# Encoder layer on one core: the second half-step's way out in seven products, its stream normed ahead by halves

## The chip, the core and the metric

One Trainium2 core runs the whole layer as one program. The metric is the time of an execution on the device in microseconds; the time before is the median of three runs. TensorE (PE) multiplies, VectorE (DVE) and ScalarE (ACT) work elementwise, GpSimd (POOL) and SyncE (SP) issue transfers (DMA) between HBM and the on-chip memory; a transfer that POOL issues may add to what lies at its destination.

## The reference

The layer works on 528 tokens (16 meta tokens ahead of 512) of width 1024; a half-step's inner width is 2816.

```python
h = concatenate([meta, x])
h = h + 0.5 * swiglu(rms_norm(h, norm_ffn1), w_ffn1_in, w_ffn1_out)
u = rms_norm(h, norm_mix) @ w_in
y = concatenate([rms_norm(rg_lru(...) * gelu(gate)), rms_norm(fourier_mix(...))])
h = h + y @ w_out
h = h + 0.5 * swiglu(rms_norm(h, norm_ffn2), w_ffn2_in, w_ffn2_out)
return rms_norm(h, norm_final)[16:]

def swiglu(h, w_in, w_out):
    gate, up = split(h @ w_in, 2)
    return (silu(gate) * up) @ w_out
```

## The kernel before

Everything lies transposed: a tile holds 128 channels by up to 528 tokens; the stream `h` is 8 such tiles. Each product of float32 numbers is done as three matmuls of split numbers (`mm3`, L240 to 246): high by high, high by low, low by high. The high part of a weight is a copy by ScalarE (L88, L221), the low part what VectorE leaves of it (L89, L222).

**Way in.** A half-step goes over 22 blocks `f` of 128 inner channels. Blocks 0 and 1 of the second are classic: 8 gate and 8 up tiles against the 8 tiles of the stream, in matmuls of 512 tokens. The others (`pair`, L398) take gate and up, and both halves of the tokens, as a 2 by 2 product and do it in seven products instead of eight, each of 4 tiles in matmuls of 256 tokens. The sums of tokens for this are made once (`sums_of_x`). The sums of weights are made per block: `pair_loads` fills raw tiles a (up, 512 KB), b (gate, 512 KB) and c (up's first half, 256 KB) by SP (L103, L104, L105), and POOL adds a half of gate onto b (L106) and the other onto c (L107). `pair_blocks` splits a, then VectorE adds c's first half onto b's second (L118) and makes c's second half (L119) from a and b:

```python
split_w(jh, jl, b[:, 512:])
nc.vector.tensor_tensor(b[:, 512:], b[:, 512:], c[:, :512], op=ALU.add)
nc.vector.tensor_tensor(c[:, 512:], a[:, 512:], b[:, 512:], op=ALU.add)
```

Raw tiles come from a pool of 7 buffers (`wraw`), split ones from 5 (`wsp`). A list of jobs gives the order of the weights; a job is split 3 ahead of its use and loaded 6 ahead. The normalisation's factor R is multiplied onto gate and up afterwards (L437, L439), as the weights don't depend on it; while it is found (`roots_of`, `rstd_of`: sums L337, root L348, reciprocal L349, spread L355), TensorE works on block 0.

**Way out.** The blocks go out in chunks (`CHUNKS2`, 4, 5, 5, 4, 4): for each of 8 output blocks d one load, one split (L221, L222), 3 matmuls of 512 tokens per block (`po`, L242 to 246) and one addition onto the stream (L517). The outputs of a chunk lie between the blocks of the next (`ffn_steps`). The last chunk is the `tail`, by groups of 256 tokens, with the final normalisation. Ahead of the half-step stands the output projection (`WOUT`, 8 steps with `pw`, L848 to 868).

The order of instructions on each engine, and the buffer that each tile gets, are set by a scheduler from the program's order; at run time every engine works its list strictly in order, and so do SP and POOL with their transfers.

Of the kernel before, what the change touches and what calls it, by code (L numbers as in the profile page):

```python
# [14 lines left out]
P = 128  # L15
D = 1024
# [10 lines left out]
CHUNKS2 = [4, 5, 5, 4, 4]  # L27
# [11 lines left out]
CS_V = [1, 2, 3]  # L39
ROOT_M = 7  # L40
# [23 lines left out]
def encoder_layer(ctx: ExitStack, tc: tile.TileContext, xT, vecs, w1i, w1o, wm, wg, wo, w2i, w2o,  # L64
# [4 lines left out]
    wraw = ctx.enter_context(tc.tile_pool(name="wraw", bufs=7))  # L69
# [63 lines left out]

    def parts_given(src):
# [14 lines left out]
    def ffn_steps(chunks, late):  # L149

        steps, f0, prev = [], 0, None
        for c in chunks:
            for i in range(c):
                steps.append(("in", f0 + i, None))
                if prev:
                    steps += [("out", prev, d) for d in range(*(max(0, ND - (c - k) * ND // c - late) if k < c else ND for k in (i, i + 1)))]
            prev = (f0, f0 + c)
            f0 += c
        return steps + [("out", prev, d) for d in range(ND)]

    STEPS1, STEPS2 = ffn_steps(CHUNKS1, 0), ffn_steps(CHUNKS2, 1)

    def ffn_jobs(wi, wo_, steps, classic):
        for kind, f, d in steps:
            if kind == "out":
                jobs.append((wo_[d][:, f[0]:f[1], :], P, f[1] - f[0], P, 8))
            elif f in classic:
                for b in range(2):
                    jobs.append((wi[f, b], P, 8, P, 2 if len(jobs) < 3 else 8))
            else:  # L170
                pair = {"src": (wi[f, 1], wi[f, 0])}
                for part in (pair_blocks, pair_sums, pair_differences):
                    jobs.append((part, pair))

    ffn_jobs(w1i, w1o, STEPS1, CLASSIC1)
# [10 lines left out]
    ffn_jobs(w2i, w2o, STEPS2, CLASSIC2)  # L186
# [13 lines left out]
    def fetch(i):  # L200
# [5 lines left out]
        elif jobs[i][0] is pair_blocks:  # L206
            pair_loads(jobs[i][1])

# [99 lines left out]
    def sums_of_x(pool, g, t0, n, k):  # L308
        m = n // 2
        a, b = h[k][:, t0:t0 + n], h[k + 4][:, t0:t0 + n]  # L310
        z = pool.tile([P, 5, HT], F32, tag="q", name="z")
        t1, t2, t3, t4, xg = [z[:, i, :m] for i in range(5)]
        nc.scalar.activation(xg, a[:, :m], AF.Copy, scale=vec(g, k))
        nc.vector.scalar_tensor_tensor(t1, a[:, m:], less(g, k), xg, op0=ALU.mult, op1=ALU.add)
        nc.vector.scalar_tensor_tensor(t2, b[:, m:], less(g, k + 4), t1, op0=ALU.mult, op1=ALU.subtract)
        nc.vector.scalar_tensor_tensor(t3, t2, -1.0, xg, op0=ALU.mult, op1=ALU.subtract)
        nc.vector.scalar_tensor_tensor(t4, b[:, :m], less(g, k + 4), t2, op0=ALU.mult, op1=ALU.subtract)
# [3 lines left out]
        return th, tl  # L321

# [17 lines left out]
    def rstd_of(q, name):  # L340
        r = tmp.tile([P, T], F32, tag="rstd", name=name)
# [26 lines left out]
    def ffn(X, g, ss, t0, n, steps, classic, on_done, tail, lead=None):  # L368
        st = {"R": ss} if lead else {}
        half = n // 2  # L370
        with tc.tile_pool(name="ffn", bufs=10) as fp, tc.tile_pool(name="ffnt", bufs=2) as ft:
# [3 lines left out]
            def sums_ready():  # L375
                if not XT:
                    XT.extend(sums_of_x(ft, g, t0, n, k) for k in range(4))

            if not lead:
                sums_ready()  # L380

            def activated(u):
                ah = fp.tile([P, T], F32R, tag="ah", name="ah")
                al = fp.tile([P, T], F32R, tag="al", name="al")
                split_to(ah[:, :n], al[:, :n], u)
                return ah, al
# [7 lines left out]
            def onto(ps, w, x, first):  # L394

                for k in range(4):
                    xh, xl = x(k)
                    mm3([ps], w[0][:, k], w[1][:, k], [xh], [xl], first and k == 0, k == 3, True)  # L398
# [3 lines left out]
            def pair(f, R):  # L402

                def new():
                    return bank("pp")[:, :half]

                add = ALU.add
                q = ft.tile([P, 5, HT], F32, tag="q", name="q")
                q0, q1, q2, u0, u1 = [q[:, i, :half] for i in range(5)]
                a11, a12, a22 = block()  # L410
                A = new()
                onto(A, a11, b(0, 0), True)
                nc.scalar.activation(q0, A, AF.Copy)  # L413
                ps = new()
                onto(ps, a12, b(1, 0), True)
                nc.vector.tensor_tensor(q0, q0, ps, op=add)
                yield
                s1, s2 = block()
                onto(A, s2, t(1), False)
                nc.scalar.activation(u0, A, AF.Copy)  # L420
                yield
                s3, s4 = block()
                C = new()
                onto(C, s3, t(2), True)
                onto(A, s1, t(0), False)
                nc.scalar.activation(q2, A, AF.Copy)
                nc.vector.tensor_tensor(u1, q2, C, op=add)
                yield
                onto(A, s4, b(1, 1), False)

                yield
                onto(C, a22, t(3), False)
                nc.vector.tensor_tensor(u0, u0, C, op=add)

                Rv = like2(R)
                uv, gv = q[:, :2, :half], q[:, 3:, :half]
                nc.vector.tensor_tensor(gv, gv, Rv, op=ALU.mult)  # L437
                nc.scalar.activation(gv, gv, AF.Silu, scale=-1.0)
                nc.vector.tensor_tensor(gv, gv, Rv, op=ALU.mult)  # L439
                nc.vector.tensor_tensor(q0, q0, u0, op=ALU.mult)  # L440
                nc.vector.tensor_tensor(q1, A, u1, op=ALU.mult)
                ah = fp.tile([P, T], F32R, tag="ah", name="ah")
                al = fp.tile([P, T], F32R, tag="al", name="al")
                split_to(like2(ah), like2(al), uv)
                acts[f] = ah, al

            late = []

            def interleaved(f, R):

                gen = pair(f, R)
                for _ in range(3):
                    next(gen)
                    if late:
                        next(late[0], None)
                if late:
                    late.pop()
                late.append(gen)

            def finish_late():  # L460
                while late:
                    for _ in late.pop():
                        pass

            def like2(x):
                return x[:, :n].rearrange("p (a b) -> p a b", a=2)

            def gate_up(pg, pu):
                R = st["R"]
                q = ft.tile([P, 5, HT], F32, tag="q", name="q").rearrange("p a b -> p (a b)")  # L470
                g, u = q[:, :T], q[:, T:2 * T]
                times(g, pg, R, n)
                nc.scalar.activation(g[:, :n], g[:, :n], AF.Silu)
                times(u, pu, R, n)
                nc.vector.tensor_tensor(u[:, :n], u[:, :n], g[:, :n], op=ALU.mult)
                return activated(u[:, :n])
# [8 lines left out]
            acts = {}  # L485
            for kind, f, d in steps:
                if kind == "in" and f not in classic:
                    interleaved(f, st["R"])
                elif kind == "in":
                    finish_late()  # L490
                    if lead and f == 0:
                        ps = lead[:2]
                    else:
# [3 lines left out]
                        if "R" in st:  # L497
                            project(ps[1])
                        else:
                            q = roots_of(ss, n, D)  # L500
                            project(ps[1], lambda: st.update(R=rstd_of(q, "r")))
                    acts[f] = gate_up(*ps)
                    sums_ready()
                elif f[1] == NF and tail is not None:
                    finish_late()
                    tail([acts[j] for j in range(*f)], ft)
                    break
                else:
                    if f[1] - 1 not in acts:
# [541 lines left out]
```

## Time and profile before

| | us |
|---|---|
| median of 3 runs (885.58 to 887.09) | 885.84 |
| the profiled execution | 885.57 |
| its span, first to last instruction | 883.8 |
| TensorE busy | 869.4 |
| VectorE busy | 667.9 |
| ScalarE busy | 454.7 |
| GpSimd busy | 68.4 |

The profile is of one execution. "Busy" of TensorE counts pipelined matmuls with modelled ends, so the time of a matmul in a row is read from start to start. VectorE's and ScalarE's rows overlap a little too. A wait is put down to what came last. 16060 instructions are recorded.

### The profile page before, as it was taken

The page shows a single profiled execution, that of the slowest core. Times are in us where ns is not written, and L with a number is a line of the kernel's source. Part 1 is how long each engine was busy: PE and PEld are TensorE (multiplying, and loading weights), DVE is VectorE, ACT ScalarE, POOL GpSimd, SP SyncE. Part 2 cuts the span into 40 slices and gives each one's busy share as a digit, 9 for nine tenths or more (in the row PEclk, how much of TensorE's full clock was granted, in tenths as well). Part 3 has the DMA queues.
Part 4 walks back from the last instruction along what each step waited for, and adds up shares of the span by engine and source line. Part 5 has one row for each costly group of instructions (what it writes and reads, how often), then busy time and mean ns, then how long its engine had stood idle before and what let it go on. Part 6 is the DMA issues. An engine that isn't in the chain of part 4 may idle for free.

```text
span 883.8 us, 16060 instructions
## 1 busy us (share of the span) xinstructions
PE 869.4 (98%) x6398; PEld 826.1 (93%) x6398; DVE 667.9 (76%) x1097; ACT 454.7 (51%) x706; POOL 68.4 (8%) x82
## 2 busy tenths in 40 slices
PE   9999999999999999999989999999999999999997
PEld 8999999999999999999977888999999999989996
DVE  7998666786776876967998689687777677767754
ACT  8755434444444443757936556455454444444434
POOL 0201100010110100000000000011110101011000
PEclk9999999999999999999999999999999999999998
DMA  8756655566566543433322333565755656546302
GB/s 298 187 134 177 156 132 131 133 144 167 122 156 165 132 108 108 129 114 107 114 73 95 93 99 72 149 169 150 182 143 139 184 126 170 155 108 168 96 1 96
DMA packets 50347, 118.84 MB, mean 134 GB/s; under 512 B 5600, under 2 KB 9440, under 8 KB 50272
## 3 DMA queue, kind: packets, MB, share of 16 engines
q1 hardware_dynamic: 38496, 96.84, 35.3%
q0 software_dynamic: 11232, 20.45, 14.7%
q8 instruction: 50, 0.82, 0.4%
q10 hardware_dynamic: 544, 0.52, 0.2%
q14 instruction: 25, 0.20, 0.1%
HBM read 115.70 MB, written 2.10 MB: 133 GB/s over the span
## 4 chain that ended last, share of the span: by engine, by line
PE 86%; DVE 9%; ACT 2%; issue 1%; DMA 1%; SPq 1%; DVEq 0%; ACTq 0%
PE pp L242 14%; PE pp L246 14%; PE pp L244 14%; PE po L242 9%; PE po L244 8%; PE po L246 8%; PE pw L244 2%; PE pw L246 2%; PE pw L242 2%; PE pm L246 1%; PE pm L242 1%; PE pm L244 1%; PE pu L242 1%; PE pu L244 1%; PE pu L246 1%
## 5 line engine op out<-in xcount | busy, mean ns | idle before, releaser
L89 DVE TENSOR_TENSOR wlo<-raw,whi 128x1024 fp32r<-128x1024 f32 x117 | 142.6, 1220 | 32.8 <-ACT whi L88 32.8
L88 ACT ACTIVATE whi<-raw 128x1024 fp32r<-128x1024 f32 x117 | 123.7, 1060 | 71.4 <-PE pp L244 38.2
L221 ACT ACTIVATE whi<-raw 128x512 fp32r<-128x512 f32 (+4 forms) x118 | 85.5, 734 | 106.7 <-PE po L244 57.6
L242 PE MATMUL pp<-th,whi 128*128 128x256 f32 (+1 forms) x468 | 132.9, 284 | 0.2 <-ACT q L413 0.2
L246 PE MATMUL pp<-xh,wlo 128*128 128x256 f32 (+1 forms) x468 | 132.3, 283 | 0.0
L246 PE MATMUL pp<-th,wlo 128*128 128x256 f32 (+1 forms) x468 | 132.1, 282 | 0.0
L244 PE MATMUL pp<-xl,whi 128*128 128x256 f32 (+1 forms) x468 | 132.0, 282 | 0.0
L242 PE MATMUL pp<-xh,whi 128*128 128x256 f32 (+1 forms) x468 | 132.0, 282 | 0.0
L244 PE MATMUL pp<-tl,whi 128*128 128x256 f32 (+1 forms) x468 | 131.9, 282 | 0.0
L242 PE MATMUL po<-ah,whi 128*128 128x264 f32 (+1 forms) x496 | 129.0, 318 | 0.3
L244 PE MATMUL po<-al,whi 128*128 128x264 f32 (+1 forms) x496 | 128.1, 316 | 0.0
L246 PE MATMUL po<-ah,wlo 128*128 128x264 f32 (+1 forms) x496 | 128.0, 315 | 0.0
L222 DVE TENSOR_TENSOR wlo<-raw,whi 128x512 fp32r<-128x512 f32 (+4 forms) x118 | 95.8, 816 | 15.0 <-ACT whi L221 14.0
L244 PEld LDWEIGHTS pp<-xl,whi 128*128 128x128 f32 x468 | 88.0, 188 | 1.0
L242 PEld LDWEIGHTS pp<-th,whi 128*128 128x128 f32 x468 | 88.0, 188 | 0.8 <-ACT q L413 0.6
L242 PEld LDWEIGHTS pp<-xh,whi 128*128 128x128 f32 x468 | 88.1, 188 | 0.8
L242 PEld LDWEIGHTS po<-ah,whi 128*128 128x128 f32 x496 | 81.5, 188 | 7.5 <-ACT ah L294 2.2
L246 PEld LDWEIGHTS pp<-xh,wlo 128*128 128x128 f32 x468 | 88.0, 188 | 0.2
L244 PEld LDWEIGHTS pp<-tl,whi 128*128 128x128 f32 x468 | 88.1, 188 | 0.0
L246 PEld LDWEIGHTS pp<-th,wlo 128*128 128x128 f32 x468 | 88.1, 188 | 0.0
L246 PEld LDWEIGHTS po<-ah,wlo 128*128 128x128 f32 x496 | 81.5, 188 | 6.2
L244 PEld LDWEIGHTS po<-al,whi 128*128 128x128 f32 x496 | 81.5, 188 | 5.3
(220 smaller groups left out, 1727.1 us busy)
## 6 DMA issues: line engine op xcount, KB each, us to landing
raw<-in_w2i SPq DMA_DIRECT2D x44, 512.0 KB, 3.8
raw<-in_w1i SPq DMA_DIRECT2D x41, 512.0 KB, 4.3
raw<-in_w2i POOLq DMA_DIRECT2D x40, 256.0 KB, 4.4
raw<-in_w1i POOLq DMA_DIRECT2D x38, 256.0 KB, 4.0
raw<-in_w1o SPq DMA_DIRECT2D x32, 256.0 KB, 2.8
raw<-in_wm SPq DMA_DIRECT2D x12, 512.0 KB, 3.6
raw<-in_w2o SPq DMA_DIRECT2D x24, 256.0 KB, 2.9
raw<-in_w2i SPq DMA_DIRECT2D x20, 256.0 KB, 3.7
```

What stands on the lines that cost most here:

```text
L88: nc.scalar.activation(hi, raw, AF.Copy)
L89: nc.vector.tensor_tensor(lo, raw, hi.bitcast(F32), op=ALU.subtract)
L221: nc.scalar.activation(hi[:p, s], raw[:p, s], AF.Copy)
L222: nc.vector.tensor_tensor(lo[:p, s], raw[:p, s], hi[:p, s].bitcast(F32), op=ALU.subtract)
L242: nc.tensor.matmul(o, wh, xh[i], start=first, stop=False, skip_group_check=go_on)
L244: nc.tensor.matmul(o, wh, xl[i], start=False, stop=False, skip_group_check=go_on)
L246: nc.tensor.matmul(o, wl, xh[i], start=False, stop=last, skip_group_check=go_on)
```

## The change

1. **The stream is normed ahead.** The last three steps of the output projection run over the first half of the tokens and then over the second. When the first half of the stream is complete, `norm_half` finds its factors and multiplies them with gain and stream (`xn`), and splits the result, while the second half is projected; the second half follows in block 0, which now runs by halves (`joined`). The multiplications by R fall away in the second half-step. The sums of tokens come from `xn` (`sums2`).
2. **Blocks 2 to 17 go out in seven products.** Chunks become 2, 4, 4, 4, 4, 4. A quad is two blocks f by two output blocks (d, d+4), two such pairs of blocks per chunk: one load of 512 KB from a new array `w2q`, four additions of VectorE for the weight sums, two splits (768 and 1024 wide), seven products of 2 tiles, four additions onto the stream (L624), and two transfers of POOL that add parts onto the stream (L636, 128 KB; L652, 256 KB). The activations of two blocks are split and summed in `squared`.
3. **The order.** After each product of the way in stands one of the way out (`schedule2`). The raw pool has 6 buffers. The tail loads two output blocks at a time. The lines of `pair_loads` move by two: L105 to L109 were L103 to L107, L120 and L121 were L118 and L119.

```diff
-CHUNKS2 = [4, 5, 5, 4, 4]
+CHUNKS2 = [2, 4, 4, 4, 4, 4]
...
-    wraw = ctx.enter_context(tc.tile_pool(name="wraw", bufs=7))
+    wraw = ctx.enter_context(tc.tile_pool(name="wraw", bufs=6))
...
+    def quad_blocks(quad):
+
+        raw = quad["raw"]
+        hi, lo = w_tiles()
+        split_w(hi[:, :768], lo[:, :768], raw[:, 256:])
+        a21, a22, a11, a12 = [raw[:, 256 * i:256 * (i + 1)] for i in range(4)]
+        nc.vector.tensor_tensor(a11, a11, a21, op=ALU.add)
+        nc.vector.tensor_tensor(a21, a21, a22, op=ALU.add)
+        nc.vector.tensor_tensor(a22, a22, a11, op=ALU.add)
+        nc.vector.tensor_tensor(a12, a12, a22, op=ALU.add)
+        return [(piece(hi, i), piece(lo, i)) for i in range(3)]
+
+    def quad_sums(quad):
+
+        hi, lo = w_tiles()
+        split_w(hi, lo, quad.pop("raw"))
+        return [(piece(hi, i), piece(lo, i)) for i in range(4)]
...
+    def schedule2():
...
+            elif j > 1:
+                new = [("so", (j - 2, prev[0], dp), name) for dp in range(4) for name in ("P1", "P2", "P6", "P7", "P5", "P4", "P3")]
...
+                for n, name in enumerate(("P1", "P2", "P6", "P7", "P5", "P4", "P3")):
+                    yield "in", f0 + i, name
+                    if i == 0 and n == 3:
+                        fill += new
+                    if j == 1:
+                        pulls = n > 2 if i == 0 else n in (0, 1, 3, 4)
+                    else:
+                        pulls = 1 + (j == len(CHUNKS2) - 1 and 0 < i < 3 and n % 2)
+                    for _ in range(min(len(fill), pulls)):
+                        yield fill.pop(0)
...
+            def squared(f):
+
+                w = wide[0]
+                b11, b21, b22, t1, t2, t3, t4 = [w[:, i] for i in range(7)]
+                hi, lo = acts_tile(f - 1, "w")
+                split_to(hi[:, :3], lo[:, :3], w[:, :3])
+                nc.vector.tensor_tensor(t1, b11, t3, op=ALU.subtract)
...
+                split_to(hi[:, 3:], lo[:, 3:], w[:, 3:])
...
+                if name == "P1":
+                    s["a22"], s["a11"], s["a12"] = block()
+                    s["A"] = new()
+                    s["q"] = tmp.tile([P, T], F32, tag="rstd", bufs=1, name="oq")[:, :half]
+                    onto(s["A"], s["a11"], y(0), True)
+                    nc.scalar.activation(s["q"], s["A"], AF.Copy, scale=0.5)
+                elif name == "P2":
+                    ps = new()
+                    onto(ps, s["a12"], y(1), True)
+                    onto_h(h1[:, :half], ps, 0.5)
+                    nc.gpsimd.dma_start(h1[:, :half], s["q"], accum_op=add)
...
+                elif name == "P4":
+                    onto(s["D"], s["a22"], y(6), False)
+                    onto_h(h2[:, :half], s["D"], -0.5)
+                    nc.gpsimd.dma_start(h2, s["v"], accum_op=add)
...
+            spread_in(rs[:, s], roots[j], P)
+            for k in range(ND):
+                x = xn[k % 4][:, 2 * (k // 4) + j]
+                nc.vector.scalar_tensor_tensor(x, h[k][:, META + j * m:META + (j + 1) * m], vec("g2", k), rs[:, s], op0=ALU.mult, op1=ALU.mult)
+                split_to(*[t[:, s] for t in X2[k]], x)
```

What this does to the order of instructions is shown at three places.

TensorE, in the middle of the second half-step: before, the end of a product of the way in (`pp`) and the first matmuls of an output block (`po`).

```order
L242 MATMUL pp_8128<-th3_6269,whi_8074 128x256
L244 MATMUL pp_8128<-tl3_6270,whi_8074 128x256
L246 MATMUL pp_8128<-th3_6269,wlo_8075 128x256
L242 MATMUL po_8246<-ah_6893,whi_8124 128x512
L244 MATMUL po_8246<-al_6894,whi_8124 128x512
L246 MATMUL po_8246<-ah_6893,wlo_8125 128x512 [waits DVE_49]
```

Now the end of a product of the way in (`th3`), then two products of a quad (`ah`, `al` are split activations, `whi`, `wlo` split weights).

```order
L332 MATMUL pp_8600<-th3_6527,whi_8498 128x256
L334 MATMUL pp_8600<-tl3_6528,whi_8498 128x256
L336 MATMUL pp_8600<-th3_6527,wlo_8499 128x256
L332 MATMUL pp_8719<-ah_7585,whi_8592 128x256
L334 MATMUL pp_8719<-al_7586,whi_8592 128x256
L336 MATMUL pp_8719<-ah_7585,wlo_8593 128x256
L332 MATMUL pp_8719<-ah_7982,whi_8592 128x256
L334 MATMUL pp_8719<-al_7983,whi_8592 128x256
L336 MATMUL pp_8719<-ah_7982,wlo_8593 128x256
L332 MATMUL pp_8786<-ah_7585,whi_8643 128x256 [waits Activation_49]
L334 MATMUL pp_8786<-al_7586,whi_8643 128x256
L336 MATMUL pp_8786<-ah_7585,wlo_8644 128x256 [waits DVE_49]
```

Where 15 matmuls of 512 tokens for an output block stood in one piece, there are now six of 256 after each product of the way in.

VectorE, around the addition that waits for POOL's transfer onto c (L118 before; `raw_8422`, `raw_8423`, `raw_8424` are a, b and c of one block). Before:

```order
L517 SCALAR_TENSOR_TENSOR hall_80<-po_8421,hall_80 128x512 [waits PE_49]
L222 TENSOR_TENSOR wlo_8452<-raw_8341,whi_8451 128x640 [waits DMAHW7_49,Activation_49]
L416 TENSOR_TENSOR q_8450<-q_8450,pp_8469 128x256 [waits PE_49,Activation_49]
L222 TENSOR_TENSOR wlo_8496<-raw_8388,whi_8495 128x640 [waits DMAHW0_49,Activation_49]
L89 TENSOR_TENSOR wlo_8537<-raw_8422,whi_8536 128x1024 [waits DMAHW1_49,PE_49,Activation_49]
L433 TENSOR_TENSOR q_8296<-q_8296,pp_8394 128x256 [waits PE_49]
L437 TENSOR_TENSOR q_8296<-q_8296,r_6341 128x2x256 [waits DVE_49]
L89 TENSOR_TENSOR jl_8541<-raw_8423,jh_8540 128x512 [waits DMAHW2_49,Activation_49]
L118 TENSOR_TENSOR raw_8423<-raw_8423,raw_8424 128x512 [waits DMASW3_49,DVE_49]
L439 TENSOR_TENSOR q_8296<-q_8296,r_6341 128x2x256 [waits Activation_49]
L119 TENSOR_TENSOR raw_8424<-raw_8422,raw_8423 128x512 [waits DVE_49]
```

The buffer of `raw_8424` (c) was that of `raw_8247`, a of the block before, whose low part `wlo_8344` stands 21 rows above L118. Now (`raw_8548` is a of one block, `raw_8743` and `raw_8744` are b and c of the next, and `raw_8744` lies in the buffer of `raw_8548`):

```order
L91 TENSOR_TENSOR wlo_8670<-raw_8548,whi_8669 128x1024 [waits Activation_49]
L91 TENSOR_TENSOR wlo_8693<-raw_8549,whi_8692 128x1024 [waits DMASW3_49,PE_49,Activation_49]
L582 TENSOR_TENSOR q_8591<-q_8591,pp_8679 128x256 [waits Activation_49]
L624 SCALAR_TENSOR_TENSOR hall_80<-pp_8719,hall_80 128x256 [waits DMASW6_49,PE_49]
L624 SCALAR_TENSOR_TENSOR hall_80<-pp_8786,hall_80 128x256 [waits DMASW1_49,PE_49]
L587 TENSOR_TENSOR q_8591<-q_8591,pp_8679 128x256 [waits PE_49]
L91 TENSOR_TENSOR jl_8877<-raw_8743,jh_8876 128x512 [waits DMAHW5_49,Activation_49]
L91 TENSOR_TENSOR wlo_8751<-raw_8550,whi_8750 128x1024 [waits PE_49,Activation_49]
L604 TENSOR_TENSOR w_8580<-q_8591 128x256 [waits Activation_49]
L605 TENSOR_TENSOR w_8580<-pp_8600,q_8591 128x256
L120 TENSOR_TENSOR raw_8743<-raw_8743,raw_8744 128x512 [waits DMASW0_49,DVE_49]
```

The row that frees the buffer, the first, now stands 10 rows above the addition that needs the new load, the last; in every other block there are 13 such rows.

TensorE and VectorE at the way into the second half-step, now: on TensorE the end of block 0's first half of tokens (`pg_6342`, `pu_6343`), the sums and the spread for the second half, and the first products of that half.

```order
L332 MATMUL pu_6343<-xh7_6124,whi_6102 128x256
L334 MATMUL pu_6343<-xl7_6125,whi_6102 128x256
L336 MATMUL pu_6343<-xh7_6124,wlo_6103 128x256
L438 MATMUL sums_6372<-ones_73,ss_4653 128x1 [waits DVE_49,PE_49]
L438 MATMUL sums_6372<-ones_73,ss_4653 128x1
L456 MATMUL rs_5876<-ident_78,root_6375 128x128 [waits DVE_49]
L456 MATMUL rs_5876<-ident_78,root_6375 128x128
L332 MATMUL pg_6342<-xh0_6110,whi_6088 128x256 [waits Activation_49]
L332 MATMUL pu_6343<-xh0_6110,whi_6102 128x256
L332 MATMUL pg_6531<-xh0_6110,whi_6106 128x512
L332 MATMUL pu_6532<-xh0_6110,whi_6344 128x512
```

On VectorE the work from the last additions onto the stream (`pw`) to that second half's scaling (`xn`).

```order
L1078 TENSOR_TENSOR hall_80<-pw_5952,hall_80 128x256 [waits PE_49]
L1078 TENSOR_TENSOR hall_80<-pw_6092,hall_80 128x256 [waits PE_49]
L1078 TENSOR_TENSOR hall_80<-pw_6093,hall_80 128x256 [waits PE_49]
L430 TENSOR_TENSOR ss_4653<-ss_4653,sq_6299 128x256 [waits Activation_49]
L312 TENSOR_TENSOR wlo_6345<-raw_6086,whi_6344 128x1024 [waits DMAHW3_49]
L430 TENSOR_TENSOR ss_4653<-ss_4653,sq_6315 128x256 [waits DVE_49,Activation_49]
L91 TENSOR_TENSOR wlo_6351<-raw_6094,whi_6350 128x1024 [waits DMAHW4_49]
L430 TENSOR_TENSOR ss_4653<-ss_4653,sq_6331 128x256 [waits DVE_49,Activation_49]
L91 TENSOR_TENSOR jl_6355<-raw_6095,jh_6354 128x512 [waits DMAHW5_49]
L450 RECIPROCAL root_6375<-root_6375 128x2 [waits Activation_49]
L120 TENSOR_TENSOR raw_6095<-raw_6095,raw_6096 128x512 [waits DMASW7_49,DVE_49]
L1072 SCALAR_TENSOR_TENSOR xn_5877<-hall_80,V_77,rs_5876 128x256 [waits PE_49]
```

Before, the same sums and spreads stood among 512-wide products of blocks 0 and 1, and no product waited for them; now the second half's products of block 0 stand behind them.

## Rows read from the trace of the kernel before

**Rows 1.** The page: span, busy us (share) per engine, TensorE's clock in tenths.

```profile
span 883.8 us, 16060 instructions
PE 869.4 (98%) x6398; PEld 826.1 (93%) x6398; DVE 667.9 (76%) x1097; ACT 454.7 (51%) x706; POOL 68.4 (8%) x82
...
PEclk9999999999999999999999999999999999999998
```

**Rows 2.** Stretch 549.36:821.31: length, busy us per engine, clock, DMA share, GB/s.

```profile
549.36:821.31 271.95, 271.86 (x1932) 254.67 (x1931) 201.79 (x309) 128.89 (x193) 30.13 (x35) 1.00 0.59 152
```

**Rows 3.** Waits of VectorE, 549 to 822 us: us in total, times, longest us.

```profile
DVE raw L118 <- DMA raw<-in_w2i: 0.7, 1, 0.7
```

**Rows 4.** Timeline of TensorE, 679 to 687 us: start, length, instruction.

```profile
679.29 0.39 PE L242 MATMUL po<-ah,whi 128*128 128x512 f32 x1
...
681.82 0.39 PE L246 MATMUL po<-ah,wlo 128*128 128x512 f32 x1
682.05 0.28 PE L242 MATMUL pp<-xh,whi 128*128 128x256 f32 x1
...
686.18 0.29 PE L246 MATMUL pp<-xh,wlo 128*128 128x256 f32 x1
```

**Rows 5.** Timelines of TensorE, ScalarE, VectorE, 530 to 537 us, by start.

```profile
530.12 0.95 PE L337 MATMUL sums<-ones,ss 128*128 128x1 f32 x8
531.10 0.26 ACT L348 ACTIVATE root<-sums,epsc 128x4 f32<-128x4 f32 x1 [2.53 <-PE sums L337]
531.40 0.18 DVE L349 RECIPROCAL root<-root 128x4 f32<-128x4 f32 x1
533.79 1.05 PE L355 MATMUL psn<-ident,root 128*128 128x128 f32 x8
534.88 0.60 ACT L362 ACTIVATE r<-psn 128x512 f32<-128x512 f32 x1 [0.76 <-PE psn L355]
536.02 0.48 DVE L314 SCALAR_TENSOR_TENSOR z<-hall,minus,z 128x256 f32<-128x256 f32 x1
```

**Rows 6.** Groups of ScalarE by form, 549:822: busy us, mean ns | idle.

```profile
L88 ACT ACTIVATE whi<-raw 128x1024 fp32r<-128x1024 f32 x54 | 57.2, 1060 | 38.5 <-PE pp L244 22.4 <-PE po L244 10.4 <-DVE raw L118 5.5
...
L426 ACT ACTIVATE q<-pp 128x256 f32<-128x256 f32 x18 | 6.6, 367 | 0.4 <-PE pp L246 0.4
```

**Rows 7.** Timeline of VectorE, 692 to 697 us.

```profile
692.96 0.42 DVE L440 TENSOR_TENSOR q<-q 128x256 f32<-128x256 f32 x1
693.30 0.42 DVE L441 TENSOR_TENSOR q<-pp,q 128x256 f32<-128x256 f32 x1
693.63 0.41 DVE L427 TENSOR_TENSOR q<-q,pp 128x256 f32<-128x256 f32 x1
693.96 1.22 DVE L89 TENSOR_TENSOR wlo<-raw,whi 128x1024 fp32r<-128x1024 f32 x1
695.10 0.68 DVE L295 TENSOR_TENSOR al<-q,ah 128x512 fp32r<-128x512 f32 x1
695.70 0.68 DVE L517 SCALAR_TENSOR_TENSOR hall<-po,hall 128x512 f32<-128x512 f32 x1
```

**Rows 8.** Line L105, the load of c by SP, whole program: issue to landing.

```profile
DMA to landing us min/median/max: 2.5/3.4/6.0
```

**Rows 9.** Line L107, the accumulation onto c by POOL, whole program: issue to landing.

```profile
DMA to landing us min/median/max: 3.7/5.0/7.1
```

**Rows 10.** Timelines of SP, POOL, VectorE, 577 to 590 us; in brackets idle before.

```profile
577.56 0.33 SPq L105 DMA_DIRECT2D raw<-in_w2i  x1
581.72 0.87 POOL L107 DMA_DIRECT2D raw<-in_w2i  x1 [4.45 <-DMA raw<-in_w2o]
588.62 0.69 DVE L118 TENSOR_TENSOR raw<-raw 128x512 f32<-128x512 f32 x1 [0.66 <-DMA raw<-in_w2i]
```

**Rows 11.** Table of stretches, 60:310 (first half-step).

```profile
60.00:310.00 250.00, 249.65 (x2040) 248.42 (x2039) 185.97 (x303) 115.20 (x169) 26.02 (x30) 1.00 0.59 147
```

**Rows 12.** Line L118, whole program: idle before it (us, times) until.

```profile
  DMA raw<-in_w2i: 0.7, 1
```

More of the change, by code (lines that the diff above doesn't have):

```diff
@@ L147, in encoder_layer, with chunk_steps @@
     jobs = []
-    def ffn_steps(chunks, late):
-        steps, f0, prev = [], 0, None
+    def chunk_steps(chunks):
+        f0, prev = 0, None
         for c in chunks:
             for i in range(c):
-                steps.append(("in", f0 + i, None))
+                yield "in", f0 + i, None
                 if prev:
-                    steps += [("out", prev, d) for d in range(*(max(0, ND - (c - k) * ND // c - late) if k < c else ND for k in (i, i + 1)))]
+                    for d in range(i * ND // c, (i + 1) * ND // c):
+                        yield "out", prev, d
@@ new lines, in encoder_layer, with ffn_jobs @@
+    STEPS1, STEPS2 = list(schedule1()), list(schedule2())
+    def ffn_jobs(wi, wo_, wq, steps):
+        pairs = {}
+        for step in steps:
+            kind, f, d = step[:3]
+            if kind == "out" and (len(step) == 3 or step[3] == 0):
+                jobs.append((wo_[d][:, f[0]:f[1], :], P, f[1] - f[0], P, 8))
+            elif kind == "tail":
+                for dp in range(ND // 2):
+                    src = wo_[2 * dp:2 * dp + 2, :, f[0]:f[1], :].rearrange("d p f m -> p d (f m)")
+                    jobs.append((src, P, 2, (f[1] - f[0]) * P, 8))
+            elif kind == "classic":
@@ L304, in gained, with split_sums @@
         return xh, xl
[L308 to L317, printed above, removed]
+    def split_sums(z, k, m):
         th = xs.tile([P, 8 * QT], F32R, tag=f"th{k}", name=f"th{k}")[:, :4 * HT].rearrange("p (i t) -> p i t", i=4)
@@ L365, in new_ss, with ffn @@
         return tmp.tile([P, T], F32, tag="ss", bufs=1, name="ss")
[L368 to L369 removed]
+    def ffn(X, R, t0, n, steps, on_done, tail, lead, sums, hook):
         half = n // 2
[L371 removed]
+        with tc.tile_pool(name="ffn", bufs=10 if lead else 3) as fp, tc.tile_pool(name="ffnt", bufs=2) as ft:
             state["pool"] = ft
@@ L376, in sums_ready, with temps @@
                 if not XT:
[L377 to L386, printed above, removed]
+                    XT.extend(sums(ft, k) for k in range(4))
+            def temps(name):
+                return ft.tile([P, 5 if lead else 4, half], F32, tag="q", name=name)
@@ L388, in b, with out_square @@
+            def out_square(f):
+                return not lead and CHUNKS2[0] <= f < NF - CHUNKS2[-1]
             def b(i, j):
@@ L394, in onto @@
             def onto(ps, w, x, first):
-                for k in range(4):
+                nk = w[0].shape[1]
+                for k in range(nk):
                     xh, xl = x(k)
[L398 to L476, printed above, removed]
+                    mm3([ps], w[0][:, k], w[1][:, k], [xh], [xl], first and k == 0, k == nk - 1, True)
```

343 lines of the change are left out of this document (286 added, 57 removed).

## Prediction

> **What bounds the kernel now.** I read the page first: TensorE is busy for 98% of the span, and the clock it was granted shows the upper level, 2.4 GHz, in every slice but the last [rows 1]. Then the table of stretches, for the stretch of the second half-step that the change rewrites, 549.36 to 821.31 us: TensorE is busy in 271.86 of 271.95 us, VectorE in 201.79 (74%), ScalarE in 128.89, and the DMA engines carry a share of 0.59 [rows 2]. So a product less is time saved, as long as no other engine becomes the bound; VectorE has 26% to spare, which is the next number to watch. Last the waits of VectorE there: for a transfer it waits only once, 0.7 us, at L118 [rows 3].
>
> The sum is made against the profiled execution's 885.57 us (span 883.8, 1.8 us around it); the median of the three runs, 885.84, is 0.27 above it. 0.2% of this, 1.8 us, is about what a measurement of this kernel can tell from no change.
>
> **Products.** Twelve 512-wide matmuls in a row start from 679.29 to 682.05, 0.230 us each; 35 steps of 256-wide ones go from 682.05 to 686.18, 0.118 each [rows 4]. Sixteen blocks go out now in 16 x 8 x 3 = 384 matmuls of 512: 88.3 us. The change does 4 chunks x 4 pairs of output blocks x 7 products x 2 x 3 = 672 of 256: 79.3 us. That is -9.0. Block 0 by halves: 96 of 256 for 48 of 512, 11.3 for 11.0, +0.3. Three steps of the output projection by halves: 144 for 72, 17.0 for 16.6, +0.4. Together **-8.3 us**, all on TensorE, which sets the end.
>
> **The way into the second half-step.** Before, the normalisation ran beside products of block 0. Now block 0 needs normed tokens. The first half's chain lies beside the second halves of the three kept steps (72 matmuls of 256, 8.5 us) and costs nothing if those cover it. The second half's does not: in the order shown, the two `sums` stand behind all of block 0's first half and ahead of its second, and nothing else is between. TensorE then waits for a chain that the trace shows in pieces: eight sums take from 530.12 to 531.10, root 0.26 and reciprocal 0.2 until 531.6, eight spreads 533.79 to 534.88 [rows 5]; then one scaling (0.48 [rows 5]), behind a 0.6 us addition of weights [rows 7], and one 256-wide copy of ScalarE (0.37) [rows 6]. With 2 sums and 2 spreads for 8 the lower sum is about 2.7, with the full rows 4.0. I take **+3.4**, between them. Bounds: 0, if the profile's chain is shorter than the matmul queue hides, and 5, if the sums of `sums2` add a microsecond. Square sums that come behind two 1.22 us weight rows on VectorE are covered by the 5.7 us of the first half.
>
> **The loop through c's buffer.** A block in seven products uses weight tiles a, b, c. c is loaded (256 KB), a transfer of POOL adds to it, and VectorE's addition (L120, before L118) waits for that. The change uses four raw tiles for every block (a, b, c and one of a quad) and has six buffers: c of the next block is the sixth tile after a of this one and gets its buffer. It may be loaded only when VectorE has done `wlo` of a. In the order before, 20 rows of VectorE lie between that row and the next L118; in the changed order there are nine in one block of two and twelve in the other, and what follows on VectorE stands behind L120, in order.
>
> Price of the work: VectorE starts the next row 1.14 us after one of 1024, 0.60 after one of 512, 0.33 to 0.34 after one of 256 (0.335 taken) [rows 7]; for 768 the middle of the first two, 0.87 (estimate). Nine rows (2 x 1.14 + 0.60 + 6 x 0.335) are 4.9 us; twelve are 6.4. The other 27 of the 48 rows of two blocks, from L120 to the row that frees the buffer, are 4.8 and 10.4, and in the first VectorE waits one copy of ScalarE (1.06 [rows 6]) for the quad's sums: 5.9 and 10.4.
>
> Price of the chain L: load 2.5 / 3.4 / 6.0 us (least, median, most), accumulation 3.7 / 5.0 / 7.1 [rows 8, 9]. From the load's issue to that of the accumulation, in the one place where VectorE waited for it, 4.16 us, which is the median load and 0.76 between; the whole there, 577.56 to 588.62, 11.06 [rows 10]. L is thus 7.0 with the least of both, 9.16 with the medians, 11.06 at the most that is seen. Loads of a and b go out right ahead of c's, as now, so I take the medians.
>
> As L is longer than 4.9 and 6.4, two blocks need 5.9 + 10.4 + 2L = 16.3 + 2L on VectorE and the queues. With L = 9.16 that is 34.6 us, against 2 x 126 matmuls of 256, 29.7. The order has this pattern in four pairs of blocks (9 to 16, about), so 4 x 4.9 = **+19.6**. At L = 7.0 it is 4 x 0.6 = 2.4, at 11.06 4 x 8.7 = 34.9. Around these pairs the rows come irregularly: four blocks before them need 30 + 3L = 57.4 us, under the 59.4 of TensorE, so nothing, but 3.7 at L = 11.06.
>
> The Trainium skill, DMA: Bandwidth & Descriptors, section "Anatomy of one DMA — SWDGE (gpsimd) path", gives a transfer of GpSimd some 2.0 us fixed and its bytes at 436 GB/s on top. By that page a 256 KB transfer would be an estimated 2.6 us, L about 6, and this loop would cost nothing (877 to 881 in all); the trace has 3.4 and 5.0 us for the two, under a load of 0.59, and I go by it.
>
> **Other edits.** Queues: POOL takes two transfers per quad more, each holding it for 0.87 us [rows 10]; L636 stands ahead of both accumulations and waits for VectorE rows that come some 2 us after the buffer is free, so with 2 x 0.87 it is through before c's load has landed: nothing, unless those rows are late, and then L grows towards its upper end. SP takes a quad's load where it took two of the way out: as many bytes. The first half-step gets six buffers for seven: there VectorE is busy in 185.97 of 250 us [rows 11] and L118 never waits for a transfer of it [rows 12], the order leaves 8.4 us of work between instead of 10.2, and its idle share stretches that to 11: nothing. VectorE in all: 26.5 us of rows and the 1.1 in two blocks of 29.7, 93%, so by itself it does not bind. The tail takes four loads of 512 KB for eight of 256: covered by the quads ahead of it; if not, one split, 1.06 + 1.14 = 2.2. At three chunk borders the first quad waits for squares: inside the same bound.
>
> Sum: 885.6 - 8.3 + 3.4 + 19.6 = **900 us**.
>
> **Rivals.** (a) *The chain is short enough, and TensorE stays the bound.* From L = 6.7 down 16.3 + 2L fits into 29.7, and the time is 877 to 881; up to L = 7.1 it is still faster by over 0.2%. For it: c's load goes out late and rather alone, and 2.5 and 3.7 occur; all that is on TensorE is certain. Against it: these are the least of all, and both accumulations of a block share POOL. (b) *They balance*: between L = 7.1 and 7.5 loop and stall take back what the products give, 884 to 887. (c) *The queue stretches the chain*: L636 comes late in every block, L stays at 11 and above: 885.6 - 8.3 + 3.4 + 34.9 + 3.7 = 919 or more. (d) *The clock falls in the waits.* In this trace TensorE hardly waits and its clock stands at 2.4 GHz up to the last slice [rows 1]. With 4.9 us of waiting in 34.6, a fall would cost nothing as long as it doubles less than 4.9 us of the 29.7; if half of the matmuls ran at 1.2 GHz, two blocks would take 29.7 + 14.9 = 44.6, and 4 x 14.9 + 880.7 is 940. By the Trainium skill, TensorE: Matmul & The Clock Gate, section "HAM oscillation — how this bites in real kernels", arrays that wait for data between groups swing between the two levels; no stretch before shows it here, as nothing waits. (e) That the change would not do what it says can be left out: the order has all 672 products and the nine and twelve rows.
>
> **How the numbers follow.** The loop at about the median chain: 0.62. (a) 0.27, (b) 0.03, (c) 0.05, (d) 0.03. So faster 0.27, same 0.03, slower 0.70. The forecast is the loop's 900. The range reaches down to (a), 877, because that holds more than 2 in 10, and up to the unknown costs at their upper bounds: 885.6 - 8.3 + 5 + 34.9 + 3.7 + 2.2 = 923; only (d) and some of (c) lie outside. The likeliest case alone is 885 to 923.
>
> **What would show it.** After: L120 with some 2 to 5 us of idle time of VectorE per block put down to a transfer in eight blocks or more, and TensorE with gaps of 2 to 3 us there; some 7 to 11 us from the issue of c's load to L120; TensorE idle for 2.5 to 4 us once between block 0's halves. Wrong would be: L120 with no such wait and TensorE busy throughout (then 877 to 881), or TensorE rows of 0.2 us and more in the middle of the half-step (the clock), or more than 0.118 us per matmul.

## Result and the profile after

The changed kernel takes 961.98 us (median of 4 runs, 958.41 to 965.53) against 885.84 before: 1.0856 times as long, 95% interval 1.0814 to 1.0899. The forecast was 900 us in 877 to 923. The direction was right, the size was not: 76 us more, where 14.7 were summed.

The page of the changed kernel, the span and parts 1 and 2:

```profile
span 959.3 us, 17078 instructions
PE 892.8 (93%) x6806; PEld 863.8 (90%) x6806; DVE 706.2 (74%) x1226; ACT 480.0 (50%) x766; POOL 96.8 (10%) x114
...
PEclk9998999999999999999999899799988989999998
```

TensorE was busy 98% of the time before [rows 1] and is now at 93%, with a lower granted clock in slices of the second half-step (a 9 is the upper level, 2.4 GHz, for nearly all of a slice; a 7 or 8 is a mean with stretches at 1.2 GHz in it). The table of stretches for the middle of the second half-step (columns as in [rows 2]) and the waits of VectorE from 545 us on:

```profile
600.00:900.00 300.00, 259.97 (x1977) 252.85 (x1977) 215.07 (x374) 139.18 (x222) 53.67 (x61) 0.93 0.61 147
```

```profile
DVE raw L120 <- DMA raw<-in_w2i: 54.7, 16, 6.1
DVE q L587 <- PE pp L336: 18.8, 11, 3.4
```

TensorE idles for 40 of 300 us, and the largest wait of VectorE is the one that stood at 0.7 us, once, in [rows 3]: L120, 16 times, 54.7 us. What stands behind L120 on VectorE waits with it; TensorE's two largest waits from 545 to 905 us are for high and low parts of weights:

```profile
PE pp L332 <- ACT whi L90: 15.7, 7, 3.7
PE pp L336 <- DVE wlo L91: 9.5, 8, 3.4
```

One turn of the loop, by the timelines of SP, POOL and VectorE (start, length, instruction, idle before):

```profile
753.83 2.35 DVE L91 TENSOR_TENSOR wlo<-raw,whi 128x1024 fp32r<-128x1024 f32 x2
```

```profile
755.08 0.33 SPq L107 DMA_DIRECT2D raw<-in_w2i  x1
```

```profile
753.44 0.87 POOL L636 DMA_DIRECT2D hall<-oq  x1 [1.40 <-ACT whi L90]
758.86 0.89 POOL L108 DMA_DIRECT2D raw<-in_w2i  x1 [4.55 <-DVE hall L624]
760.49 0.88 POOL L109 DMA_DIRECT2D raw<-in_w2i  x1 [0.74 <-DVE q L570]
```

```profile
766.76 0.69 DVE L120 TENSOR_TENSOR raw<-raw 128x512 f32<-128x512 f32 x1 [4.48 <-DMA raw<-in_w2i]
```

The first of the two `wlo` rows frees the buffer (it is a's), the load of c goes out at 755.08, the accumulation at 760.49, and VectorE stands still for 4.48 us until 766.76: 11.7 us from the load's issue. Two blocks of this stretch, from one L120 (728.87) to the next but one:

```profile
728.87:766.76 37.89, 33.78 (x260) 33.00 (x258) 27.29 (x48) 17.83 (x28) 7.04 (x8) 0.91 0.63 148
```

48 rows of VectorE, 27.29 us of work, 37.89 us of time. The accumulation onto c (L109, whole program) takes longer than in [rows 9]:

```profile
DMA to landing us min/median/max: 3.8/6.0/9.2
```

The first half-step waits too, once, at the place where seven buffers had been enough (timeline of VectorE, 87 us):

```profile
87.45 0.69 DVE L120 TENSOR_TENSOR raw<-raw 128x512 f32<-128x512 f32 x1 [4.50 <-DMA raw<-in_w1i]
```

From there on the additions at L120 stand about 6 us behind those of before, to the end of the half-step. And the way into the second half-step (timeline of TensorE, between the halves of block 0):

```profile
538.12 0.28 PE L336 MATMUL pu<-xh,wlo 128*128 128x256 f32 x1
539.88 0.58 PE L438 MATMUL sums<-ones,ss 128*128 128x1 f32 x4 [1.48 <-DVE ss L430]
541.01 1.22 PE L456 MATMUL rs<-ident,root 128*128 128x128 f32 x4 [0.55 <-DVE root L450]
543.26 0.58 PE L332 MATMUL pg<-xh,whi 128*128 128x256 f32 x1 [1.02 <-ACT xh L384]
```

5.0 us from the last product of the first half to the first of the second (538.24 with a step of 0.12 to 543.26), where 3.4 were taken and 5 was the bound.

### The profile page after: what moved, and what is told of

Read it like the earlier page. It is cut to its first block, busy times and chain, and to the rows that moved or that the text cites. A ratio compares the mean times of both kernels' runs of the same rounds, so it can differ in the third digit from the quotient of the medians.

```text
span 959.3 us, 17078 instructions
## 1 busy us (share of the span) xinstructions
PE 892.8 (93%) x6806; PEld 863.8 (90%) x6806; DVE 706.2 (74%) x1226; ACT 480.0 (50%) x766; POOL 96.8 (10%) x114
## 5 line engine op out<-in xcount | busy, mean ns | idle before, releaser
L90 ACT ACTIVATE whi<-raw 128x1024 fp32r<-128x1024 f32 (+1 forms) x149 | 151.0, 1032 | 126.4 <-DVE raw L149 51.1
L91 DVE TENSOR_TENSOR wlo<-raw,whi 128x1024 fp32r<-128x1024 f32 (+1 forms) x149 | 175.2, 1193 | 26.9 <-ACT whi L90 25.0
L311 ACT ACTIVATE whi<-raw 128x512 fp32r<-128x512 f32 (+3 forms) x95 | 69.4, 740 | 69.6 <-PE po L334 36.4
L312 DVE TENSOR_TENSOR wlo<-raw,whi 128x512 fp32r<-128x512 f32 (+3 forms) x95 | 78.0, 826 | 12.2 <-ACT whi L311 11.3
L332 PE MATMUL pp<-ah,whi 128*128 128x256 f32 x224 | 66.7, 298 | 21.4 <-ACT whi L90 15.5
L332 PE MATMUL po<-ah,whi 128*128 128x264 f32 (+1 forms) x368 | 79.3, 295 | 2.3 <-ACT ah L384 2.2
L334 PE MATMUL po<-al,whi 128*128 128x264 f32 (+1 forms) x368 | 79.9, 295 | 1.1 <-DVE al L385 1.1
L336 PE MATMUL po<-ah,wlo 128*128 128x264 f32 (+1 forms) x368 | 78.6, 293 | 0.0
L336 PE MATMUL pp<-ah,wlo 128*128 128x256 f32 x224 | 66.8, 299 | 9.5 <-DVE wlo L91 9.5
L334 PE MATMUL pp<-al,whi 128*128 128x256 f32 x224 | 66.0, 295 | 5.1 <-DVE al L385 5.0
```

Of the source, the lines that this page charges most:

```text
L90: nc.scalar.activation(hi, raw, AF.Copy)
L91: nc.vector.tensor_tensor(lo, raw, hi.bitcast(F32), op=ALU.subtract)
L311: nc.scalar.activation(hi[:p, s], raw[:p, s], AF.Copy)
L312: nc.vector.tensor_tensor(lo[:p, s], raw[:p, s], hi[:p, s].bitcast(F32), op=ALU.subtract)
L332: nc.tensor.matmul(o, wh, xh[i], start=first, stop=False, skip_group_check=go_on)
L334: nc.tensor.matmul(o, wh, xl[i], start=False, stop=False, skip_group_check=go_on)
```

## The experiments

**1. The kernel before with six raw buffers.**

```diff
-    wraw = ctx.enter_context(tc.tile_pool(name="wraw", bufs=7))
+    wraw = ctx.enter_context(tc.tile_pool(name="wraw", bufs=6))
```

> The kernel before with six raw buffers for seven and nothing else. Theory (c's buffer is what the changed kernel waits for): the first half-step loses what it lost in the changed kernel, about 6 us between 84 and 108 us, with one wait of VectorE of some 4 us at L118; in the second half-step seven rows for c's buffer leave 7 to 9 us of VectorE's work between its release and L118, near the chain's 9 to 11, so some microseconds more: 892 to 905 in all. Rival (the first half-step's loss comes from its products written in another order): the time stays 885 to 887.

893.21 us, 1.0065 (1.0048 to 1.0082) of before: inside the theory's range, at its lower end. Waits of VectorE at L118 for transfers are now:

```profile
DVE raw L118 <- DMA raw<-in_w2i: 12.3, 9, 2.8
DVE raw L118 <- DMA raw<-in_w1i: 3.6, 1, 3.6
```

Six buffers cost the old order 6 us, and nearly all of that in the first half-step. In the second the nine waits of 12.3 us cost little: L118 stands 4.9 us behind the kernel before at block 3 (549.36 there) and 5.5 at block 19 (792.77 there).

```profile
554.22 0.68 DVE L118 TENSOR_TENSOR raw<-raw 128x512 f32<-128x512 f32 x1
798.28 0.69 DVE L118 TENSOR_TENSOR raw<-raw 128x512 f32<-128x512 f32 x1
```

So a wait of VectorE at this row is not yet lost time.

**2. The changed kernel with seven raw buffers, one buffer for jh and jl.**

```diff
-    wraw = ctx.enter_context(tc.tile_pool(name="wraw", bufs=6))
+    wraw = ctx.enter_context(tc.tile_pool(name="wraw", bufs=7))
...
-        jh = state["pool"].tile([P, 512], F32R, tag="jh", name="jh")
-        jl = state["pool"].tile([P, 512], F32R, tag="jl", name="jl")
+        jh = state["pool"].tile([P, 512], F32R, tag="jh", bufs=1, name="jh")
+        jl = state["pool"].tile([P, 512], F32R, tag="jl", bufs=1, name="jl")
```

> The changed kernel with seven raw buffers (the room comes from one buffer for two of the split tiles jh and jl). The order then leaves 14 to 17 us of VectorE's work between the release of c's buffer and L120. Theory: no wait at L120, TensorE's clock back at the upper level through the second half-step, the first half-step as before; only the way into the second half-step stays some 8 us longer than before, so 883 to 892. Rival 1 (the quads' additions and splits fill VectorE): L120 does not wait but TensorE waits for low parts of weights, 900 to 930. Rival 2 (the transfers onto the stream and the clock are the cause): over 940, with the clock still low.

1005.13 us: over the 940 of rival 2, but not by its cause, as the second half-step's clock is up (0.99). The single buffers of jh and jl hit the first half-step, where a block's last product that reads them runs beside the next block (the first row), while in the second half-step TensorE is nearly always busy (the second). Stretches 60 to 310 and 600 to 850 us:

```profile
60.00:310.00 250.00, 206.81 (x1453) 201.32 (x1452) 130.90 (x210) 76.45 (x118) 18.27 (x21) 0.88 0.39 103
600.00:850.00 250.00, 243.47 (x1820) 230.38 (x1819) 205.05 (x368) 133.38 (x218) 37.62 (x43) 0.99 0.57 141
```

The run as a whole says nothing; its second half-step pointed to the clean version, number 5.

**3. VectorE adds gate onto c.** In the second half-step the transfer L109 is replaced by one VectorE row; six buffers.

```diff
+        if pair["second"]:
+            nc.vector.tensor_tensor(c[:, :4], c[:, :4], b[:, :4], op=ALU.add)
...
-        nc.gpsimd.dma_start(c[:, :4], gate[:, :4], accum_op=ALU.add)
+        if not pair["second"]:
+            nc.gpsimd.dma_start(c[:, :4], gate[:, :4], accum_op=ALU.add)
```

> The changed kernel, but in the second half-step VectorE adds gate onto c (128x512, one row of 0.6 us per block) and POOL's transfer onto c is gone; c's buffer is still a's of the block before. Theory (the chain of load and accumulation behind that buffer): the chain shrinks from about 10.5 us to the loads, 4 to 5 us, of which 3.3 to 3.6 lie beside VectorE's work, and two blocks take 30 to 32 us for 38: about 905 to 925, first half-step and way in unchanged. Rival (a fuller VectorE or the transfers onto the stream): 950 to 975.

901.13 us, 4 below the theory's range and 61 less than the change with the same buffers: a chain without its accumulation is worth 61 of the 76 us. 600 to 850 us:

```profile
600.00:850.00 250.00, 244.63 (x2001) 240.25 (x1999) 224.06 (x398) 141.94 (x224) 40.04 (x46) 0.99 0.63 161
```

**4. VectorE adds the quads' parts onto the stream.**

```diff
-                    nc.gpsimd.dma_start(h1[:, :half], s["q"], accum_op=add)
+                    nc.vector.tensor_tensor(h1[:, :half], h1[:, :half], s["q"], op=add)
...
-                    nc.gpsimd.dma_start(h2, s["v"], accum_op=add)
+                    nc.vector.tensor_tensor(h2, h2, s["v"], op=add)
```

> The changed kernel with VectorE, not POOL's transfers, adding the two parts of a quad onto the stream (one row of 256 and one of 512 per quad, about 0.95 us). Theory: c's chain stays, its load to L120 9 to 11 us where the buffer comes late, and the time stays near the change's, 945 to 970 (the order of VectorE's rows moves, so some microseconds either way). Rival (the transfers onto the stream hold POOL's queue and lengthen the chain): the chain falls to 8 to 9 us and the time under 930.

959.35 us (before beside it 886.96), as the theory had it. The wait at L120 and the accumulation's time stay without a single transfer onto the stream:

```profile
DVE raw L120 <- DMA raw<-in_w2i: 58.6, 14, 7.1
```

```profile
DMA to landing us min/median/max: 3.6/6.1/9.2
```

So rival (c) of the prediction, the queue stretched by L636, is not the cause. What makes the accumulation slower than before was not found.

**5. Seven raw buffers, jh and jl single in the second half-step only.** As number 2, but jh and jl have two buffers in the first half-step (`state["j"] = 2 if lead else 1`, where lead is set in the first half-step alone).

> The changed kernel with seven raw buffers, the room taken in the second half-step alone (one buffer each for jh and jl there; the first half-step keeps two). Theory (the wait for c's buffer took some 70 us, six buffers in the first half-step 6): no wait at L120 in the second half-step, the granted clock there 0.98 or more, the first half-step as before, the way into the second half-step still 8 to 9 us longer; 877 to 887. Rival (VectorE is full at 27 of 29.7 us per two blocks and cannot be fed in time): 895 to 920 with TensorE waiting for low parts of weights.

891.84 us, 1.0063 (1.0046 to 1.008) of before: 70 us below the change, 5 above the theory's range and 3 under the rival's. No wait at L120 is left in the second half-step; the accumulations take 4.7 us in the median of the whole program, and the clock is up. 600 to 850 us:

```profile
600.00:850.00 250.00, 246.94 (x2047) 243.49 (x2046) 221.01 (x387) 145.57 (x230) 53.55 (x61) 1.00 0.74 179
```

**6. The way out alone.** As number 5, but output projection, block 0 and the factors R as before (two more 512-wide rows of VectorE per block).

```diff
+                if not lead:
+                    nc.vector.tensor_tensor(gv, gv, like2(R[0]), op=ALU.mult)
```

> Seven raw buffers and the way out in seven products, but the stream is not normed ahead: the output projection and block 0 run as in the kernel before, and gate and up are multiplied by the factors (two more VectorE rows of 512 per block). Theory (products save 9.0 us, the way in through halves costs 8 to 9, six buffers the rest): 876 to 882. Rival (1.2 us more of VectorE per block bind, 28.9 of 29.7 per two blocks with waits): 886 to 900.

886.18 us (10 runs), 0.9992 (0.998 to 1.0004): no difference, at the lower edge of the rival's range. From the first product of block 2 to the end it takes 333.7 us (550.9 to 884.6) for 335.3 before (548.55 to 883.8), 1.6 less where 9.0 were summed. Part of the rest is TensorE at rest where the first squares meet the last classic outputs, and VectorE near full:

```profile
560.00:650.00 90.00, 87.30 (x671) 82.55 (x670) 79.21 (x136) 46.74 (x73) 14.91 (x17) 1.00 0.60 158
600.00:850.00 250.00, 247.56 (x2047) 243.92 (x2046) 236.97 (x417) 144.95 (x229) 54.48 (x62) 1.00 0.71 173
```

Without counting 600 to 650 us twice, that is 3.2 us of TensorE at rest. The remainder shows when its rows are read from start to start. The 256-wide matmuls from block 2 on are as short as taken, 0.118 us in the median, but 79 of 2352 take over 0.138, 10.3 us more in all (the 3.2 included); before, it was 4 of 1680 and 0.7 us. So the products are saved, and short waits take them back. The profile puts some of these waits down to parts of weights from ScalarE and VectorE; for most it names no releaser.

**7. Norm ahead alone, jh and jl single.** As number 5 with the old way out (`CHUNKS2 = [4, 5, 5, 4, 4]`, `out_square` false, P3 and P4 of a block beside the next one, as in the first half-step).

> Seven raw buffers, the stream normed ahead by halves as in the change, but the second half-step's way out as in the kernel before (chunks 4, 5, 5, 4, 4, matmuls of 512, one addition each); one buffer for jh and jl in the second half-step. Theory (the way in costs 8 to 9 us, nothing comes back, as VectorE was not the bound): 892 to 897, with the waits of TensorE between the halves of block 0. Rival (less work for VectorE shortens the half-step): 880 to 888.

1025.19 us, neither. In the order of that way out the single buffers do to the second half-step what they did to the first in number 2 (560 to 650 us: TensorE busy 73.42 of 90), so the question stayed open until number 10.

**8. Blocks 0 and 1 by halves.**

```diff
                 for j in range(2):
                     s = slice(j * half, (j + 1) * half)
-                    for k in range(ND):
-                        hook(j, k)
...
+                    for e in range(0, len(ps), 2):
+                        for k in range(ND):
+                            if e == 0:
+                                hook(j, k)
```

> As the run with seven raw buffers (second half-step only), but blocks 0 and 1 both run their first half of tokens before the second half of either, so 42 matmuls of 256 (5 us) stand between the spread and the second half. Theory (TensorE waits there for the second half's chain): 4 to 6 us less than that run, 872 to 882. Rival (VectorE's scaling and splitting of the second half, some 6 us, is late all the same): within 2 us of that run.

896.64 us, 5 more than number 5, which neither theory nor rival had. TensorE's wait ahead of the second half falls from 5 us to the 1.5 for the sums, but the sums of tokens were put behind a low part whose split buffer comes free with block 0's end:

```profile
550.19 1.23 DVE L91 TENSOR_TENSOR wlo<-raw,whi 128x1024 fp32r<-128x1024 f32 x1 [6.20 <-ACT whi L90]
```

**9. As 8, the sums of tokens ahead of those weights.**

```diff
+                    if j:
+                        sums_ready()
                     for e in range(0, len(ps), 2):
```

> As the run with blocks 0 and 1 by halves (seven raw buffers), but the sums of tokens for the seven-product blocks are written right after the second half is normed, ahead of the weights that wait for a split buffer. In the run before they came 12 us later and TensorE waited some 10 us for them and what stood behind, between 550 and 600 us. Theory (that delay is the miss): 8 to 12 us less than that run, 884 to 889. Rival (six microseconds of scaling and splitting are too much for VectorE at that place in any order): 893 and above.

887.64 us, 1.0008 (0.9994 to 1.0023), 9 less than number 8, as the theory had it: the order of VectorE was its miss. It is the best form of the whole change, 74 us below the change and not to be told from the kernel before.

**10. Norm ahead alone, jh and jl double.** As number 7, with two buffers each and room from five pairs of activations for six.

> The stream normed ahead, way out as before, seven raw buffers, and now two buffers each for jh and jl in both half-steps. Theory (the way in costs 8 to 9 us; c's buffer has 8 to 9 us of VectorE's work between, so a few short waits at L120 on top): 893 to 903, the granted clock 0.98 or more. Rival (norming ahead itself is what stalls the half-step, as the run with one buffer had it): over 950.

893.93 us, 1.0078 (1.0055 to 1.0102), in the theory's range: norming ahead by halves costs 7 us by itself. In its second half-step L120 waits for no transfer.

**11. More products.** Six buffers; in the second half-step two overwritten matmuls ahead of each accumulation group.

```diff
+HEAT = 2
...
+                if first and not lead:
+                    for _ in range(HEAT):
+                        nc.tensor.matmul(ps, w[0][:, 0], x(0)[0], start=True, stop=False, skip_group_check=True)
```

> The changed kernel (six buffers) with 12 matmuls of 256 more per block, which are overwritten by what follows: 1.4 us more of TensorE per block, 28 us in the half-step, and less time at rest. VectorE's work between the release of c's buffer and L120 is 4.9 and 5.2 us for 4.9 and 6.4. Theory (the loop through c's buffer sets the time, TensorE and its clock do not): 955 to 975. Rival 1 (TensorE's work sets it): 985 to 995. Rival 2 (the lower level of the clock after the waits sets it, and busier it stays up): 925 to 945.

999.12 us, beyond all three. The clock stayed at 0.91 to 0.94 (four stretches from 560 to 950 us), and c's accumulation, now mostly the third of a burst of POOL's, takes over 8 us in nine blocks, where two did in the change. Timeline of POOL (the row of L110 is c's accumulation, which landed at 821.50):

```profile
811.44 0.89 POOL L640 DMA_DIRECT2D hall<-oq  x1 [8.21 <-DMA raw<-in_w2i]
812.15 1.09 POOL L109 DMA_DIRECT2D raw<-in_w2i  x1
812.98 1.15 POOL L110 DMA_DIRECT2D raw<-in_w2i  x1
```

As the kernel moved the chain itself, it does not tell what the clock costs.

## Why the prediction was right and wrong

**The loop: right in kind, mis-sized in both factors.** The order told which buffer c waits for and that VectorE would stand at L120; numbers 3 and 5 show that this is where the time goes (61 and 70 us back). VectorE's work was right: 48 rows were summed as 26.5 us and take 27.29. The chain was not. The step that failed is "so I take the medians", L = 9.16: by L107's issue to L120 in the ten blocks between 687 and 881 us it is 9.4 to 10.8 in one block and 11.2 to 11.7 in the other, 21.4 for a pair. With the 16.3 us of VectorE's side, as summed, that is 37.7, and the pair takes 38.7 us ((880.92 - 687.51) / 5) for a summed 34.6. The medians came from loads that mostly had time to spare; the bound of 11.06, from the one place where VectorE waited, was the better row for a loop in which it always does.

**The count failed with it.** "Four pairs of blocks" and "so nothing" for the blocks around them: there were five pairs at 9.0 us over TensorE's 29.7, 45 us, and from block 3 to block 10 L120 falls back by 19 us more (20.9 to 40.2 behind the kernel before; in number 5 it stands 23.8 behind at both). The four blocks ahead of the pairs failed by the same term:

```profile
583.49 0.69 DVE L120 TENSOR_TENSOR raw<-raw 128x512 f32<-128x512 f32 x1 [1.38 <-DMA raw<-in_w2i]
650.06 0.69 DVE L120 TENSOR_TENSOR raw<-raw 128x512 f32<-128x512 f32 x1 [6.05 <-DMA raw<-in_w2i]
```

From block 4 to block 8 that is 66.6 us. The prediction's own 30 + 3L gives 66.1 with the chains of blocks 5, 6 and 8 (11.0, 13.9 and 11.2 us), for 57.4 with the medians; number 5 takes 55.6 there (585.16 to 640.74). So the sum was set up rightly, and L was too short in it.

Number 5 has as many matmuls as the changed kernel, 6806. Counted off one by one, the change stands 5.4 us behind it through the rest of the first half-step (329.6 for 324.2), 25.8 at 691 us, 61.5 at 885 and 69 at the end: about 5 from the first half-step, 20 from the blocks ahead of the five pairs, 36 from the pairs and 8 from what follows.

**"Nothing" for the first half-step** was wrong by 5 to 6 us: the order left 7.3 us of VectorE's work at block 7 (75.66 to 82.95), not 8.4, with hardly any idle time in it, and there the chain was 11.8 (75.66 to 87.45). Number 1 shows it as the buffers' doing, in the kernel before.

**The way in:** +3.4 with 0.7 of matmuls were taken; number 10 has 7.0, and number 5 against 6 5.7. The weight rows on VectorE, said to be covered, were not: the sums of squares stand behind two of them, and TensorE waits 1.48 us for them; the rest is the chain at 3.5, as summed.

**Products, -8.3.** Not seen in the time of any version. The matmuls go at the rate taken, two blocks of number 6 take 30.2 us for 29.7, but number 6 as a whole gains nothing that can be measured: its 79 longer steps, 10.3 us, are more than the 9.0. "All on TensorE, which sets the end" left them out.

**Rivals.** (a) a short chain: wrong here; with seven buffers L120 does not wait, but the time is 892 and not 877. (c) the queue: number 4 leaves the wait in place without those transfers. (d) the clock: it fell, to 0.93 in the stretch above, with 1.00 in number 5, and the sign named for it came: of some 1960 steps of 256-wide matmuls from 600 to 900 us, 171 take 0.20 to 0.26 us. A mean of 0.93 over 300 us can have cost at most some 21 us (7%), and the change falls back by over 60 us behind number 5 there. The Trainium skill, TensorE: Matmul & The Clock Gate, section "HAM oscillation — how this bites in real kernels", has such swings where the array waits for data, and the trace agrees (0.93 with TensorE at rest for 40 of 300 us, 1.00 with 3 of 250 in number 5). How much of the 21 us it did cost is not settled. In the pair shown VectorE waits 3.38 us for a product (740.48), and yet L120 behind it still waits 0.73 us for the transfer, so there it cost nothing; and chain and rows leave 1.0 us of a pair's 38.7 for all else. The Trainium skill, DMA: Bandwidth & Descriptors, section "Anatomy of one DMA — SWDGE (gpsimd) path", has a fixed and a per-byte time for a transfer of GpSimd, an estimated 2.6 us for 256 KB; these accumulations, with 6.0 in the median, do not agree, and the measurement decides.

## What to carry to other kernels

Count for each tile that a transfer fills how much work lies, in the order of the engine that frees its buffer, between the release and its first use, and set that against the whole chain of transfers at its longest. Where it is shorter, the engine waits. Whether the waits cost time shows in the whole turn, the chain and the engine's work from the first use back to the release: where that is longer than the bounding engine's time for the same blocks, as in the change (37.7 us for a pair against 29.7), the loss comes back in every turn, and a spare buffer is worth more than what it was given up for. In number 1, where the blocks kept their pace, waits of 12.3 us cost about 0.7. Price the chain from the places where the engine did wait for it. When one part of a change costs memory, measure the parts with the memory given back first.

## What was not expected

The time of c's accumulation, always 256 KB, follows neither the DMA share nor its place behind other transfers of POOL. Over the whole program its median is 4.7 us in number 5 and 6.0 in the change, though from 600 us on the DMA share is 0.74 there and 0.61 here. Third in flight behind two others it took 5.2 to 6.4 us in five blocks of the change (700 to 854 us), 3.7 to 4.8 in six of number 5, and over 7.3 in ten of thirteen of number 11; in number 5 those with none ahead of them took longer, 6.6 to 7.6 in seven blocks (627 to 812 us). What sets it stays open.

And one buffer less for a half-size tile (jh, jl) cost 113 us in the first half-step (1005.13 in number 2, 891.84 in number 5) and 131 in the second (1025.19 in number 7, 893.93 in number 10), where a block's last products on it run beside the next block; where they do not, in the second half-step of number 5, ScalarE's idle time ahead of jh for those products is 22.3 us from 560 to 880 us, against 23.0 in the changed kernel with two buffers.
